# A retrieval layer's walk over 128 expert blocks: split-float matmuls against plain float32, and gathered rows on TensorE against VectorE

## The chip, the cores and the metric

One NeuronCore of a Trainium2 chip runs the whole program. The metric is the device time in microseconds (us) of one execution. PE is TensorE (matmuls; PEld is its weight load), DVE is VectorE, ACT is ScalarE, POOL is GpSimd, SP is SyncE, which here only issues DMAs. "Block" below is a block of 128 experts.

## The reference

Tokens go through a token mixer and a layer norm (not touched here), then through a PEER layer: each token picks 8 x 16 of 16384 experts by two top-16 searches, and its output is a gated sum over them.

```python
def peer_ffn(x, wq, sub_keys, u_tab, v_tab):        # x (512, 1024), tables (16384, 1024) float32
    ...
    s_top, i_top = lax.top_k(scores, PEER_TOPK)
    cand_s = ...; cand_i = i_top[half 0] * 128 + i_top[half 1]
    best_s, best_pos = lax.top_k(cand_s, PEER_TOPK)
    expert_idx = jnp.take_along_axis(cand_i, best_pos, axis=-1)   # (512, 8, 16)
    gates = jax.nn.softmax(best_s, axis=-1)
    def chunk(args):
        xc, ec, gc = args
        u = jnp.take(u_tab, ec, axis=0)
        act = jax.nn.gelu(jnp.einsum("cd,chkd->chk", xc, u)) * gc
        vv = jnp.take(v_tab, ec, axis=0)
        return jnp.einsum("chk,chkd->cd", act, vv)
    ...
x = layer_norm(ALPHA * x + peer_ffn(x, ...), ln2_g, ln2_b)
```

## The kernel before, in words

Everything is float32. The kernel treats the two halves of the 512 tokens in different ways, side by side.

**Dense half (tokens 256 to 511).** A walk over the 128 blocks computes, per block, H = u_block x (a 128x256 result over eight 128-deep steps), its gelu, the product with the block's gates, and adds (gated gelu)^T v_block to four accumulators of 128x512. Each block's u and v (512 KB each) are loaded by SP. A float32 matmul is replaced by three matmuls on split operands, a high part (`fp32r`) and a low part: ACT copies the high part, DVE subtracts for the low part (`split`, lines 115 and 118). So H takes 24 matmuls (`h_run`, L1261) and the output side 12 (`v_tile`, L1253). The first blocks are different already: the output side of blocks 0 to 30 (`NATV = 31`) uses plain float32 on the raw tile (L1243), and H of blocks 6 to 23 does too (`ramp_fill`, L703, with a plain copy of x made by `native_x`). H of the first 24 blocks (`RAMP`) is computed in the ramp, ahead of the walk: between the routing instructions and in the gate stage below.

**Gates of the dense half.** They are made as matmuls of one-hot rows, 32 blocks by 16 tokens at a time: `g_hot` makes four one-hot tensors on DVE, `g_token` 32 small matmuls per group on PE (L972, L973), `g_out` copies them to a ring of 56 blocks on ACT. The first 32 blocks' gates are made in a stage of their own before the walk (16 groups), the other 48 groups in three windows of blocks (`GWIN`: 14 to 31, 38 to 62, 70 to 94) between the walk's matmuls.

**Sparse half (tokens 0 to 255).** Rows of u and v are gathered by indirect DMAs that POOL issues (L1037), 128 rows of 4 KB each. For u, one gather holds slot j of 128 tokens, and DVE forms the 128 dot products in one instruction (`sparse_u`, L1042). For v, one gather holds the 128 slots of one token (`idxT`), and PE adds them up: `sparse_v` multiplies four gathers at a time by columns of coefficients (`expand`, L1102), 8 matmuls of 512 columns. There are 256 gathers of u and 256 of v.

**Order.** Every engine works through its instructions as the program writes them. `work(b, share)` hands a quota of sparse items to block b: 5 a block up to block 13, 3.5 up to block 30, then 383 over 95 blocks, 4.03 a block. `pull` issues gathers as long as fewer than `NGAT = 9` row buffers are held:

```python
    def pull():
        while gq and held[0] < NGAT:
            kind, i, j = gq.popleft()
            t = spare()
            ...
            held[0] += 1
```

A gather therefore waits, on POOL's queue, until the instruction that used the buffer's former content is done. PE meets in block b: H of block b+1, the sparse matmuls that fall there, then the output side of block b, which needs `af` of block b (`a_mul`, L1004, on DVE, behind whatever DVE has in front of it).

## Time and profile before

| what | value |
|---|---|
| device time, 3 runs | 1423.62 us median (1423.08 to 1429.82) |
| the profiled execution | 1420.93 us, its span 1419.1 us |
| PE busy | 1322.5 us, 93% of the span |
| DVE busy | 1086.8 us, 77% |
| POOL busy | 779.0 us, 55% |
| ACT busy | 512.5 us, 36% |
| bytes moved | 439.83 MB, mean 310 GB/s |
| mean granted clock of TensorE | 0.977 of full speed |

The span lasts from the first to the last instruction; the device time has 1.8 us more around it. Busy time of PE includes overlaps of pipelined matmuls, so a busy PE need not be working at its peak. The first 320 us are the mixer and the routing, the walk goes from about 411 to 1392 us.

### The profile page before, as it was taken

The numbers are of one execution on the slowest core, as the hardware profiler recorded it, in microseconds if no ns is written. First come the engines' busy times: TensorE is split into PE (matmuls) and PEld (weight loads), VectorE is DVE, ScalarE is ACT, GpSimd is POOL, SyncE is SP. The second block draws the span as 40 slices with busy tenths as digits, with TensorE's granted clock in tenths as the row PEclk, the third lists the DMA queues.
The fourth block names the chain that finished last, engine by engine and source line by source line (L and its number), as shares of the span: only waits on it lengthen the run. The fifth ranks groups of instructions, "written<-read, shape, count | busy, mean of one in ns | idle before, by whom it ended". The sixth has DMA issues, their size and how long they took to land.

```text
span 1419.1 us, 24250 instructions
## 1 busy us (share of the span) xinstructions
PE 1322.5 (93%) x9229; PEld 1006.2 (71%) x9229; DVE 1086.8 (77%) x2292; ACT 512.5 (36%) x735; POOL 779.0 (55%) x687
## 2 busy tenths in 40 slices
...
GB/s 212 186 63 13 134 84 128 83 75 110 229 199 389 420 411 367 378 375 375 413 377 392 388 385 390 405 419 404 405 403 402 406 364 416 402 419 409 419 408 141
DMA packets 125444, 439.83 MB, mean 310 GB/s; under 512 B 14480, under 2 KB 16528, under 8 KB 125328
## 3 DMA queue, kind: packets, MB, share of 16 engines
...
q14 instruction: 44, 0.36, 0.1%
...
## 4 chain that ended last, share of the span: by engine, by line
PE 50%; issue 14%; DMA 13%; POOL 11%; DVE 10%; ACT 2%; POOLq 0%; DVEq 0%; SPq 0%; ACTq 0%
PE acc L1253 12%; PE w L1261 11%; POOL gat L1037 10%; DMA gat<-in_v,idxT 8%; PE facc L1102 8%; DMA gat<-in_u,idx 4%; PE b L138 4%; PE b L139 4%; PE b L137 4%; PE w L703 3%; DVE i_top L757 2%; DVE s_top L755 1%; PE z L312 1%; DVE sc L760 1%; DVE gat L1042 1%
## 5 line engine op out<-in xcount | busy, mean ns | idle before, releaser
L1037 POOL DMA_INDIRECT gat<-in_u,idx x256 | 336.5, 1314 | 222.5 <-DVE gat L1042 142.6
L1037 POOL DMA_INDIRECT gat<-in_v,idxT x256 | 280.6, 1096 | 178.6 <-PE facc L1102 100.1
L1042 DVE SCALAR_TENSOR_TENSOR gat<-gat,x1s 128x1024 f32<-128x1024 f32 x256 | 309.4, 1222 | 15.7 <-DMA gat<-in_u,idx 15.1
L1253 PE MATMUL acc<-vh,A 128*128 128x512 f32 x768 | 261.5, 401 | 0.0
L1261 PE MATMUL w<-x1Tdh,whi 128*128 128x256 f32 x832 | 241.7, 291 | 1.6 <-ACT gl L1264 1.4
L1261 PE MATMUL w<-x1Tdl,whi 128*128 128x256 f32 x832 | 235.2, 283 | 0.0
L1261 PE MATMUL w<-x1Tdh,wlo 128*128 128x256 f32 x832 | 234.9, 282 | 0.0
L118 DVE TENSOR_TENSOR vl<-vraw,vh 128x1024 fp32r<-128x1024 f32 x96 | 117.5, 1224 | 121.2 <-ACT vh L115 121.1
L1253 PEld LDWEIGHTS acc<-vh,A 128*128 128x128 f32 x768 | 145.1, 189 | 81.5 <-issue 28.5
L1243 PE MATMUL acc<-vraw,af 128*128 128x512 f32 x248 | 136.9, 697 | 48.6 <-DVE af L1004 45.2
L115 ACT ACTIVATE whi<-wraw 128x1024 fp32r<-128x1024 f32 (+1 forms) x146 | 151.0, 1036 | 48.6 <-DMA wraw<-in_wq 25.5
L1102 PE MATMUL facc<-gat,expand 128*32 128x512 f32 x1024 | 152.5, 600 | 14.8 <-DMA gat<-in_v,idxT 14.1
L1261 PEld LDWEIGHTS w<-x1Tdh,whi 128*128 128x128 f32 x832 | 159.4, 192 | 6.1 <-ACT gl L1264 2.3
L1261 PEld LDWEIGHTS w<-x1Tdl,whi 128*128 128x128 f32 x832 | 159.3, 191 | 2.4
L1261 PEld LDWEIGHTS w<-x1Tdh,wlo 128*128 128x128 f32 x832 | 159.0, 191 | 0.0
L118 DVE TENSOR_TENSOR wlo<-wraw,whi 128x1024 fp32r<-128x1024 f32 (+1 forms) x109 | 131.7, 1210 | 34.7 <-ACT whi L115 34.0
L115 ACT ACTIVATE vh<-vraw 128x1024 fp32r<-128x1024 f32 x96 | 101.4, 1056 | 143.5 <-issue 118.1
L1253 PE MATMUL acc<-vl,A 128*128 128x512 f32 x384 | 151.0, 393 | 0.0
L118 POOL TENSOR_TENSOR wlo<-wraw,whi 128x1024 fp32r<-128x1024 f32 x37 | 92.5, 2504 | 96.0 <-ACT whi L115 96.0
L1243 PEld LDWEIGHTS acc<-vraw,af 128*128 128x128 f32 x248 | 51.1, 219 | 112.3 <-DVE af L1004 61.2
L115 ACT ACTIVATE ring<-w 128x384 f32<-128x384 f32 (+2 forms) x80 | 52.4, 740 | 169.4 <-PE w L973 169.4
L1264 ACT ACTIVATE gl<-w 128x256 f32<-128x256 f32 x104 | 39.9, 384 | 185.3 <-PE w L1261 182.8
...
## 6 DMA issues: line engine op xcount, KB each, us to landing
wraw<-in_uT SPq DMA_DIRECT2D x128, 512.0 KB, 8.4
vraw<-in_v SPq DMA_DIRECT2D x128, 512.0 KB, 6.5
wraw<-in_w_in SPq DMA_DIRECT2D x18, 512.0 KB, 3.8
wraw<-in_wq SPq DMA_DIRECT2D x16, 512.0 KB, 3.9
wo<-in_w_out SPq DMA_DIRECT2D x8, 512.0 KB, 9.3
gat<-in_u,idx POOLq DMA_INDIRECT x256, 8.3
gat<-in_v,idxT POOLq DMA_INDIRECT x256, 6.9
...
```

What stands on the lines that cost most here:

```text
L115: return act.activation(o, i, AF.Copy, scale=scale)
L118: eng.tensor_tensor(out=o, in0=a, in1=b, op=OP.subtract)
L137: pe.matmul(ps, lh, rh, start=start, stop=False)
L138: pe.matmul(ps, lh, rl, start=False, stop=False)
L139: pe.matmul(ps, ll, rh, start=False, stop=stop)
L703: pe.matmul(ramp[1], uraw[b][:, k, :], native["x"][:, k, :], start=k == 0, stop=k == 7)
L1037: pool.indirect_dma_start(out=t, out_offset=None, in_=table, in_offset=bass.IndirectOffsetOnAxis(ap=idx, axis=0))
L1042: dve.scalar_tensor_tensor(t, t, 1.0, x1s[i], op0=OP.mult, op1=OP.mult, accum_out=dots[:, j:j + 1])
L1102: pe.matmul(facc[hf][32 * j:32 * j + 32, :], expand[:, j, o:o + 32], ts[j][:, 512 * hf:512 * hf + 512], start=r == 0, stop=r == 31)
L1243: pe.matmul(acc[hf], af[b][:, c:c + 128], raw[:, 512 * hf:512 * hf + 512], start=b == 0, stop=False)
L1253: pe.matmul(acc[hf], lhs[x], rhs[y], start=b == 0 and p == 0, stop=b == NI - 1 and p == 2)
L1261: pe.matmul(ps, w[:, k, :], x1Td[x][:, k, :], start=k == 0 and p == 0, stop=k == 7 and p == 2)
```

## The change

Six things change together.

1. **H of the walk** uses the raw u tile and a plain copy of x: 8 float32 matmuls instead of 24. The splits of u in the walk are gone. `native_x` now writes the plain copy over the split copy of x, so that only blocks 0 to 4 (`RSPL = 5`) use the split one; the rest of them is finished ahead of `native_x`.
2. **The output side** uses the raw v tile for all 128 blocks: 4 float32 matmuls instead of 12. The splits of v and of `af` (the tile `A2`) are gone.
3. **v rows of the sparse half** are gathered by slot like those of u, with the same index tile, and DVE adds coefficient times row to the residual in place (`sparse_v`). `idxT`, its transposes, `expand`, the transposed coefficients and the accumulators `facc` are gone; ACT scales the residual by ALPHA once.
4. **Row buffers** are a list of 18 (12 own ones, four former split tiles, two from the low part of x) and 20 once the ramp's gelu tiles are used up. v has three raw buffers instead of two, and there are two PSUM banks each for H and for gates.
5. **Order in a block**: `a_mul(b)` stands in block b for blocks from 24 on (before: `a_mul(b+1)` in block b, for every block).
6. **Routing**: POOL writes the looked-up products in the order in which they are added up, and DVE adds both of them with one `tensor_reduce` (`add_up`) over adjacent elements; `add_half` is gone. `g_out` writes 16 adjacent tokens at a time.

```diff
-RSPL = 6
+RSPL = 5
-NGAT = 9
-EH = 16
+NGAT = 12
-NATV = 31
...
     def native_x():
...
+            pss.append(ps)
+        x, rows = [xtp.tile([128, 8, ND], FR, name=n).bitcast(F32) for n in ("x1Tdh", "x1Tdl")]
+        for i, ps in enumerate(pss):
+            copy_act(x[:, 2 * i:2 * i + 2, :], ps)
+        native["x"], native["rows"] = x, rows
...
-            pool.tensor_tensor(out=pr, in0=ge, in1=delta[:, :, :, None].to_broadcast([128, NB, TOPK, TOPK]), op=OP.mult)
+            pool.tensor_tensor(out=pr.rearrange("p t s a -> p t a s"), in0=ge, in1=delta[:, :, :, None].to_broadcast([128, NB, TOPK, TOPK]), op=OP.mult)
...
-                dve.tensor_reduce(out=dst, in_=pr.rearrange("p t a s -> p t s a"), axis=AX.X, op=OP.add)
+                dve.tensor_reduce(out=dst, in_=pr, axis=AX.X, op=OP.add)
...
         def route_e(h, pr):
-            add_half(i2A[:, :, h, :], pr)
+            add_up(i2A[:, :, h, :], pr)
...
+        ramp_fill(8 * RSPL - ramp[0])
         native_x()
         ramp_fill(TFILL[0])
...
+    for n in ("whi", "wlo"):
+        for _ in range(2):
+            free.append(wts.tile([128, 8, 128], FR, name=n, bufs=2).bitcast(F32).rearrange("p a c -> p (a c)"))
+    for i in range(2):
+        free.append(native["rows"][:, 4 * i:4 * i + 4, :].rearrange("p a c -> p (a c)"))
+    for i in range(NGAT):
+        free.append(gp.tile([128, D], F32, name=f"gat{i}"))
 
     def pull():
-        while gq and held[0] < NGAT:
+        while gq and free:
...
+    def sparse_v(i, j):
+        t = gats.pop(("v", i, j))
...
+        dve.scalar_tensor_tensor(x1s[i], t, coef[i][:, j:j + 1], x1s[i], op0=OP.mult, op1=OP.add, **more)
...
+        free.append(t)
...
     def v_tile(b, i, slots):
...
         for hf in range(2):
-            cc = slice(512 * hf, 512 * hf + 512)
-            rhs = (vh[:, cc], vl[:, cc])
-            for p, (x, y) in enumerate(((0, 0), (0, 1), (1, 0))):
-                pe.matmul(acc[hf], lhs[x], rhs[y], start=b == 0 and p == 0, stop=b == NI - 1 and p == 2)
-                slots()
+            pe.matmul(acc[hf], af[b][:, c:c + 128], raw[:, 512 * hf:512 * hf + 512], start=b == 0, stop=b == NI - 1)
+            slots(3)
 
     def h_run(b, slots):
-        ps = hbank[:, :ND]
-        (wh, wl) = usplit.pop(b)
+        ps = hbank[b % 2][:, :ND]
+        raw = uraw.pop(b)
         for k in range(8):
-            for p, (w, x) in enumerate(((wh, 0), (wh, 1), (wl, 0))):
-                pe.matmul(ps, w[:, k, :], x1Td[x][:, k, :], start=k == 0 and p == 0, stop=k == 7 and p == 2)
-                slots()
+            pe.matmul(ps, raw[:, k, :], native["x"][:, k, :], start=k == 0, stop=k == 7)
+            slots(3)
...
-        if b + 2 >= RAMP:
-            u_split(b + 2)
-            u_load(b + 4)
+        if b + 3 >= RAMP:
+            u_load(b + 3)
         work(b, 0.25)
-        v_split(b + 1)
-        if b >= NATV:
-            v_load(b + 3)
+        if b >= RAMP:
+            a_mul(b)
...
-        a_mul(b + 1)
-        a_high(b + 1)
+        if b + 1 < RAMP:
+            a_mul(b + 1)
...
-        if b < NATV:
-            v_load(b + 2 + (b == NATV - 1))
+        v_load(b + 3)
```

Three places in the order of instructions, before and after. Names before the arrow are what is written, behind it what is read; line numbers are each kernel's own.

**DVE, about ten blocks before the end of the walk.** Before, two blocks:

```order
L1004 SCALAR_TENSOR_TENSOR af<-gl,ring 128x256
L118 TENSOR_TENSOR A_12402<-af,A_12402 128x256
L118 TENSOR_TENSOR wlo<-wraw,whi 128x1024
L118 TENSOR_TENSOR vl<-vraw,vh 128x1024
L1004 SCALAR_TENSOR_TENSOR af<-gl,ring 128x256
L118 TENSOR_TENSOR A_12473<-af,A_12473 128x256
L118 TENSOR_TENSOR wlo<-wraw,whi 128x1024
L118 TENSOR_TENSOR vl<-vraw,vh 128x1024
```

After, somewhat over two blocks (L1064 is `sparse_v`, L985 is `a_mul`; `whi`, `wlo` and `gat_...` are row buffers):

```order
L985 SCALAR_TENSOR_TENSOR af<-gl,ring 128x256
L1064 SCALAR_TENSOR_TENSOR x1s_85<-gat_3734,coef_4503,x1s_85 128x1024
L1064 SCALAR_TENSOR_TENSOR x1s_85<-glx,coef_4503,x1s_85 128x1024 x2
L1064 SCALAR_TENSOR_TENSOR x1s_85<-gat_3738,coef_4503,x1s_85 128x1024
L985 SCALAR_TENSOR_TENSOR af<-gl,ring 128x256
L1064 SCALAR_TENSOR_TENSOR x1s_85<-gat_3735,coef_4503,x1s_85 128x1024
L1064 SCALAR_TENSOR_TENSOR x1s_85<-whi,coef_4503,x1s_85 128x1024 x2
L1064 SCALAR_TENSOR_TENSOR x1s_85<-wlo,coef_4503,x1s_85 128x1024
L985 SCALAR_TENSOR_TENSOR af<-gl,ring 128x256
L1064 SCALAR_TENSOR_TENSOR x1s_85<-gat_3736,coef_4503,x1s_85 128x1024
L1064 SCALAR_TENSOR_TENSOR x1s_85<-gat_3737,coef_4503,x1s_85 128x1024
L1064 SCALAR_TENSOR_TENSOR x1s_85<-wlo,coef_4503,x1s_85 128x1024
```

Two 128x1024 subtractions and one 128x256 subtraction a block go, about four 128x1024 steps on gathered v rows come.

**PE, late in the walk**, from the end of H of one block to the first part of the next output side. Before (L1102 are the sparse matmuls):

```order
L1261 MATMUL w<-x1Tdh,whi 128x256
L1261 MATMUL w<-x1Tdl,whi 128x256
L1261 MATMUL w<-x1Tdh,wlo 128x256
L1102 MATMUL facc_4540<-gat,expand 32x512 x4
L1102 MATMUL facc_4541<-gat,expand 32x512 x4
L1253 MATMUL acc_0_4536<-vh,A_13753 128x512
L1253 MATMUL acc_0_4536<-vl,A_13753 128x512
L1253 MATMUL acc_0_4536<-vh,A_13753 128x512
L1253 MATMUL acc_1_4537<-vh,A_13753 128x512
L1253 MATMUL acc_1_4537<-vl,A_13753 128x512
```

After, one and a half blocks: H, output side, H (`h_...` and `w` are its two banks), output side:

```order
L1199 MATMUL h_4512<-x1Tdh,wraw 128x256 x8
L1192 MATMUL acc_0_4507<-vraw,af 128x512
L1192 MATMUL acc_1_4508<-vraw,af 128x512
L1192 MATMUL acc_0_4509<-vraw,af 128x512
L1192 MATMUL acc_1_4510<-vraw,af 128x512
L1199 MATMUL w<-x1Tdh,wraw 128x256 x8
L1192 MATMUL acc_0_4507<-vraw,af 128x512
L1192 MATMUL acc_1_4508<-vraw,af 128x512
L1192 MATMUL acc_0_4509<-vraw,af 128x512
L1192 MATMUL acc_1_4510<-vraw,af 128x512
```

The sparse matmuls are gone from PE, and each three matmuls on split parts are one on raw tiles.

**POOL, from the first gather on.** Before:

```order
L1037 DMA gat<-in_u,idx_1552 128x1024 x128
L1037 DMA gat<-in_u,idx_1553 128x1024 x9
L1091 MEMSET expand 128x2172
L1037 DMA gat<-in_u,idx_1553 128x1024 x3
L1037 DMA gat<-in_v,idxT 128x1024 x4
L1037 DMA gat<-in_u,idx_1553 128x1024 x4
L1037 DMA gat<-in_v,idxT 128x1024 x4
L1037 DMA gat<-in_u,idx_1553 128x1024 x4
```

After:

```order
L1008 DMA whi<-in_u,idx_1552 128x1024 x2
L1008 DMA wlo<-in_u,idx_1552 128x1024 x2
L1008 DMA x1Tdl<-in_u,idx_1552 128x1024 x2
L1008 DMA gat_3727<-in_u,idx_1552 128x1024
L1008 DMA gat_3728<-in_u,idx_1552 128x1024
L1008 DMA gat_3729<-in_u,idx_1552 128x1024
```

Nine more, each into a `gat_` buffer of its own, follow directly: the first 18 gathers now find a free buffer instead of the first nine, and the v gathers take the same index tile as those of u.

## Rows read from the trace of the kernel before

**Rows 1.** The page of the profiled execution: busy time, share of the span and number of instructions of each engine (part 1).

```profile
PE 1322.5 (93%) x9229; PEld 1006.2 (71%) x9229; DVE 1086.8 (77%) x2292; ACT 512.5 (36%) x735; POOL 779.0 (55%) x687
```

**Rows 2.** Busy time by stretch, all engines. Columns: stretch and its length, then busy us (and instructions) of PE, PEld, DVE, ACT and POOL, the granted clock of TensorE, the mean busy share of the 16 DMA engines, GB/s.

```profile
205.00:260.00 55.00, 53.79 (x462) 53.59 (x462) 49.73 (x300) 22.88 (x30) 41.86 (x53) 1.00 0.40 129
260.00:317.00 57.00, 50.12 (x417) 48.67 (x415) 56.28 (x327) 16.90 (x25) 41.14 (x55) 1.00 0.26 81
369.00:411.00 42.00, 42.00 (x623) 37.64 (x621) 35.67 (x64) 18.97 (x23) 16.83 (x9) 1.00 0.67 226
411.00:514.00 103.00, 65.36 (x113) 25.25 (x112) 87.11 (x153) 0.38 (x1) 80.91 (x66) 0.83 0.97 384
514.00:638.00 124.00, 111.65 (x855) 70.75 (x856) 120.62 (x208) 29.55 (x50) 81.88 (x61) 0.93 0.99 378
638.00:1148.00 510.00, 491.68 (x3817) 380.01 (x3815) 419.24 (x647) 210.07 (x312) 318.31 (x256) 1.00 1.01 398
1178.00:1392.00 214.00, 214.00 (x1454) 156.44 (x1447) 92.59 (x112) 78.69 (x114) 104.81 (x107) 1.00 1.02 410
1392.00:1419.00 27.00, 13.62 (x81) 10.29 (x79) 15.66 (x33) 8.44 (x15) 0.00 (x0) 0.79 0.19 75
```

**Rows 3.** The same view for line 1004 (`a_mul`, one instruction a block) alone: DVE busy time and, in brackets, how many blocks lie in each stretch; clock, DMA share, GB/s.

```profile
411.00:514.00 103.00, 5.93 (x14) 0.83 0.97 384
514.00:638.00 124.00, 7.12 (x17) 0.93 0.99 378
638.00:1148.00 510.00, 26.84 (x64) 1.00 1.01 398
1148.00:1392.00 244.00, 13.17 (x31) 1.00 1.01 404
```

**Rows 4.** The same view, all engines, for a stretch of 20 us in which the transfers run fastest.

```profile
1160.00:1180.00 20.00, 19.39 (x116) 12.19 (x117) 5.51 (x8) 5.46 (x8) 8.62 (x10) 1.00 1.03 419
```

**Rows 5.** Instructions of PE in order of time, one block late in the walk. Columns: start us, duration us, line, operation, out<-in, shapes, how many in a row.

```profile
1182.46 0.28 PE L1261 MATMUL w<-x1Tdh,whi 128*128 128x256 f32 x1
...
1185.42 1.92 PE L1102 MATMUL facc<-gat,expand 128*32 128x512 f32 x16
1187.27 0.50 PE L1253 MATMUL acc<-vh,A 128*128 128x512 f32 x1
...
1190.12 0.28 PE L1261 MATMUL w<-x1Tdh,whi 128*128 128x256 f32 x1
```

**Rows 6.** Instructions of PE in order of time: plain float32 matmuls of H in the ramp (L703) and of the output in the walk (L1243), each recorded as two instructions, and a bunch of 16 gate matmuls (L972, L973) with the matmul behind it.

```profile
360.53 3.62 PE L703 MATMUL w<-x1Tsh,wraw 128*128 128x256 f32 x16
363.99 0.38 PE L900 MATMUL b<-ident,sc 128*128 128x128 f32 x2
...
593.17 3.60 PE L1243 MATMUL acc<-vraw,af 128*128 128x512 f32 x8
...
1003.63 0.20 PE L972 MATMUL w<-ohAg,ohB 128*128 128x32 f16 x1
...
1004.19 0.36 PE L1261 MATMUL w<-x1Tdh,whi 128*128 128x256 f32 x1
```

**Rows 7.** Instructions of DVE in order of time inside a gate window: the four one-hot instructions of one group of tokens, a step on a gathered u row with its accumulator read, and `a_mul`.

```profile
1019.63 1.22 DVE L957 TENSOR_TENSOR ohB<-i2T,iota 128x2048 f16<-128x2048 f16 x1
1021.90 1.22 DVE L1042 SCALAR_TENSOR_TENSOR gat<-gat,x1s 128x1024 f32<-128x1024 f32 x1
1023.04 0.42 DVE L1004 SCALAR_TENSOR_TENSOR af<-gl,ring 128x256 f32<-128x256 f32 x1
1023.38 1.22 DVE L1042 SCALAR_TENSOR_TENSOR gat<-gat,x1s 128x1024 f32<-128x1024 f32 x1
```

**Rows 8.** Groups of equal instructions: line, engine, operation, out<-in, shapes, count, busy us, mean ns of one, idle time before and what ended it. A 128x1024 step with a scalar pointer (L1134), the subtractions that the splits leave on DVE (L118), and, of the routing, a strided reduction (L799), the first of four halvings (L805) and a contiguous reduction (L908).

```profile
L1134 DVE SCALAR_TENSOR_TENSOR x1s<-x1s,fs,gat 128x1024 f32<-128x1024 f32 x2 | 2.6, 1286 | 2.3 <-ACT gat L1125 2.3
L118 DVE TENSOR_TENSOR wlo<-wraw,whi 128x1024 fp32r<-128x1024 f32 x105 | 129.1, 1230 | 33.2 <-ACT whi L115 32.4 <-PE acc L1253 0.5
L118 DVE TENSOR_TENSOR vl<-vraw,vh 128x1024 fp32r<-128x1024 f32 x96 | 117.5, 1224 | 121.2 <-ACT vh L115 121.1
L799 DVE TENSOR_REDUCE pki<-pr 128x64 int32<-128x1024 f32 x8 | 15.3, 1917 | 0.0
L805 DVE TENSOR_TENSOR pr<-pr 128x512 f16<-128x512 f16 x8 | 7.8, 972 | 0.0
L908 DVE TENSOR_REDUCE sm<-sc 128x32 f32<-128x512 f32 x1 | 0.7, 678 | 0.0
```

**Rows 9.** Gathers issued by POOL, in order of time (start, duration, and in square brackets the idle time before and what ended it): in the gate stage, at the start of the walk, late in the walk.

```profile
387.09 1.96 POOL L1037 DMA_INDIRECT gat<-in_u,idx  x1 [0.30 <-issue]
413.02 1.68 POOL L1037 DMA_INDIRECT gat<-in_u,idx  x1 [23.98 <-DVE gat L1042]
...
1206.77 0.93 POOL L1037 DMA_INDIRECT gat<-in_v,idxT  x1 [0.30 <-issue]
1210.60 0.93 POOL L1037 DMA_INDIRECT gat<-in_v,idxT  x1 [2.90 <-PE facc L1102]
```

**Rows 10.** Busy time of POOL on line 1037 (gathers) in the first 14 blocks: POOL us (instructions), clock, DMA share, GB/s.

```profile
411.00:514.00 103.00, 80.91 (x66) 0.83 0.97 384
```

**Rows 11.** Waits of PE, the largest: what waited, line, what for; us in total, times, longest.

```profile
PE acc L1243 <- DVE af L1004: 45.2, 17, 8.1
```

**Rows 12.** The page's DMA issues (part 6): out<-in, queue, count, KB each, median us from issue to landing.

```profile
vraw<-in_v SPq DMA_DIRECT2D x128, 512.0 KB, 6.5
```

208 lines of the change are left out of this document (71 added, 137 removed).

## The prediction

> **What bounds the kernel now.** I read the shares first, then the busy time stretch by stretch, then single blocks. PE's 93% of the span [rows 1] is a mean over stages with different limits. In the gate stage (369 to 411) PE is busy all 42.00 us [rows 2]. The blocks are counted by `a_mul` [rows 3]. Blocks 0 to 13 (411 to 514) are not PE's: 65.36 of 103 us. DVE has 87.11 us, and POOL 80.91 us in 66 gathers; with the 0.30 us of issue ahead of each [rows 9] that is 80.91 + 66 x 0.30 = 101 of 103 us [rows 2, 10]. POOL is full because it starts late: the tenth gather goes out at 413.02, after 23.98 us of waiting for a u step to free one of nine buffers [rows 9]. The transfers run at 384 GB/s there, against 419 at their best [rows 2, 4]. Blocks 14 to 30 take 124 us with DVE at 120.62. Blocks 31 to 94 take 510 us, 7.97 a block, with PE at 491.68; blocks 95 to 125 take 244 us, 7.87 a block, with PE busy for 214.00 of the 214 us to 1392 [rows 2, 3]. There PE is the bound; its late block lasts 1190.12 - 1182.46 = 7.66 us: H 2.96, sparse matmuls 1.85, output side 2.85 [rows 5]. The transfers stand close behind, at 398 and 404 to 410 GB/s [rows 2, 3].
>
> **The change, part by part.** The sum goes against the profiled execution, 1420.9 us, which is 2.7 below the median of the three runs.
>
> *PE.* In plain float32 eight H matmuls take 363.99 - 360.53 = 3.46 us, and the output side of a block 3.60 us with its modelled end [rows 6]; I take 3.44, the pitch H shows, since both have the same number of columns. The walk's PE block becomes 6.90 us (7.06 at most) instead of 7.66: the two float32 parts cost 1.1 us more and the 1.85 us of sparse matmuls go. A group of gates adds two bunches of 1004.19 - 1003.63 = 0.56 us, about 1.2 with their gaps [rows 6]; 32 groups lie in blocks 31 to 94.
>
> *DVE.* The subtractions go (117.5 and 129.1 us [rows 8], mostly in the walk) and 256 v steps come. No v step is in this trace; the nearest rows are a u step, 1.22 us long at a pitch of 1023.04 - 1021.90 = 1.14 us [rows 7], and a step with a scalar pointer, 1.286 us [rows 8]. I take 1.25, range 1.14 to 1.29, and `a_mul` at 0.34 and four one-hot instructions at 2.27 [rows 7]. Blocks 0 to 30 hold 129 sparse items, all u but one. Blocks 31 to 94 hold 258, half of them v.
>
> *Transfers.* Bytes stay the same, 4.03 + 2 pieces of 0.524 MB in a late block = 3.16 MB, but nine more gathers (4.7 MB) leave in the gate stage, where only 226 GB/s run [rows 2]. At the gate stage's pitch of 1.96 + 0.30 us [rows 9] eighteen gathers take 41 us of its 42.
>
> *Stage by stage.*
> - Routing and gate stage. The strided reduction (1917 ns) becomes contiguous; from 678 ns for half the elements [rows 8] I estimate 1.36 us: 0.56 less, eight times. Four halvings (972 ns and at most half as much again and again, under 1.94 us) become one such reduction: up to 0.6 less, eight times. PE's idle time between 205 and 317, 1.2 + 6.9 us [rows 2], bounds the gain at 8 us. Against it: one split H block becomes plain (+0.5 us), PE waits for ACT's copies over `x1Tdh` before the fill matmuls (no row shows it; 0 if they keep ahead of PE, 3 if it waits for most of the four), and POOL's product of the same size writes strided, which may cost nothing or double its 2 us a head. Value -3, ends -8 and +8.
> - Blocks 0 to 30, 227 us now. Floors after: transfers 103 x 0.384 + 124 x 0.378 = 86.4 MB, less 4.7, at 418 GB/s = 195 us; DVE 129 x 1.14 + 31 x 0.34 + 16 x 2.27 = 194 us; PE in blocks 14 to 30, where eight H are due, 17 x 3.44 + 8 x 3.46 + 16 x 1.2 = 105 us at full clock, 113 at the granted 0.93 [rows 2]. POOL has 111 gathers left at 1.5 us (103 / 66), 167 us, and is no bound. Three near-equal floors never overlap wholly: 204, or -23 (ends 197 and 215).
> - Blocks 31 to 94, 510 us now. PE 64 x 6.90 + 32 x 1.2 = 480 (490 with 7.06). Transfers 510 x 0.398 = 203 MB, 484 us at 419 GB/s, 495 at 410. DVE 127 x 1.14 + 131 x 1.25 + 64 x 0.34 + 32 x 2.27 = 403. Value 490, or -20 (ends 482 and 510).
> - Blocks 95 to 125, 244 us now. Transfers 244 x 0.404 = 98.6 MB, 235 us at 419, 240 at 410; PE 31 x 6.90 = 214; DVE 125 x 1.25 + 31 x 0.34 = 167. The transfers are the bound: 237, or -7 (ends 233 and 244).
> - Tail, 27 us: the last H and output sides at plain pitch and no split to prepare, finish steps as before: +3 (ends 0 and +5).
>
> Sum -3 - 23 - 20 - 7 + 3 = -50: 1371 us by the profile, 1372 asked for here. What hides the loss of 1.1 us a block on PE's float32 parts is the removed 1.85 us of sparse matmuls; without that cover blocks 31 to 125 would cost 95 x 1.1 = 105 us. `a_mul(b)` now stands in block b behind about four DVE steps, so a late gathered row holds DVE, then `a_mul`, then the output side queued on PE, and every H behind it; v raw has three buffers, so `v_load` is next in line to be late.
>
> **The rivals.**
>
> *R1, transfers alone.* If 18 to 20 buffers keep the queues full, everything after the gate stage runs at 419 GB/s: 389 MB less 4.7 is 917 us, from 408 to 1325, and 28 us of tail: 1353; with 8 us gained in the routing, 1345. For it: the late stretches reach 410 to 419 already [rows 2, 4]. Against: PE needs as long in blocks 31 to 94.
>
> *R2, coupling.* PE lost 45.2 us to `af` in the early blocks [rows 11]. If the order in a block costs PE 0.3 to 0.5 us for `af` in each of 95 blocks, 29 to 48 us return: 1395 to 1420. For it: `a_mul` behind gathered rows. Against: `af` has three buffers, and DVE has a fifth of its time free.
>
> *R3, slower: POOL's gathers get slow.* A gather's issue costs 0.93 us late in the walk, with little on DVE, and 1.68 to 1.96 at the start of the walk and in the gate stage [rows 9], where DVE is busy for 85% [rows 2]. After the change DVE runs v steps with two tensor inputs all through the walk. At the gate stage's 2.26 us a gather, 383 gathers take 866 us in blocks 31 to 125 instead of 754, and 111 take 251 in blocks 0 to 30: 408 + 251 + 866 + 30 = 1555. It decides above (1419 - 408 - 30) / 494 = 1.99 us a gather. Against: in blocks 0 to 13, with DVE at 85%, the pitch is 1.5, and 4.03 x 1.5 = 6.0 us a block is under 7.5; the subtractions that go had two inputs as well and took about as long. The Trainium skill bears on this (SBUF — State Buffer, "SBUF: two separate sides"): DVE with two SBUF inputs, against a GpSimd instruction that reads SBUF, and GpSimd take one port pair as an exclusive lock, held for a whole instruction, while the other blocks fully. Read strictly, each gather could wait out a whole v step, and the time would be the one just given. The trace agrees in kind, 0.93 against 1.96 us, but does not show a full step added at the 1.5 us pitch.
>
> *R4, slower: a dear v step.* If the in-place sum took over (781 - 250) / 254 = 2.09 us, DVE's 127 x 1.14 + 95 x 0.34 + 32 x 2.27 = 250 us and 254 v steps would eat all gains (781 = 754 and the 27 us gained elsewhere). Against: the nearest rows say 1.29 at most.
>
> *R5, slower: loads behind gathers.* With 18 gathers queued, a u or v load could land late; v loads land in 6.5 us [rows 12], and one issued three blocks (22 us) ahead has room to spare. It would need more than 15 us.
>
> **How the numbers follow.** My forecast 0.60 (1355 to 1393, likeliest 1372), R1 0.17 (1338 to 1355), R2 0.13 (1393 to 1425), R3 0.05 (1450 to 1555), R4 and R5 together 0.05 (1425 to 1480). A measurement here can tell 0.5%, 7 us, from no change: faster (below 1416) 0.60 + 0.17 + 0.09 = 0.86, same 0.04, slower 0.10. The range 1343 to 1408 leaves out about 0.04 below and 0.16 above, which is where R2's end and the slower cases lie.
>
> **What the profile after would show.** Right: eighteen gathers back to back before the walk; block 0 at about 408, block 31 at 612, block 95 at 1102, the end of block 125 at 1339; transfers at 410 to 419 GB/s from the first block to the last; PE at 6.9 us a block; v steps of 1.14 to 1.29 us; POOL's gathers at 1.0 to 1.5 us. Wrong: PE waiting for `af` in most late blocks (R2); POOL full at 2 us a gather and DVE waiting for rows that were issued late (R3); DVE full with v steps of 2 us (R4); PE waiting for `wraw` or `vraw` (R5); a first block after 411 would void the routing term.

## The result, and the profile after

The changed kernel takes 1366.76 us, the median of 4 runs (1364.74 to 1369.49), against 1424.42 us (1423.08 to 1429.82) of the kernel before: a ratio of 0.9588, 95% interval 0.9558 to 0.9618. The profiled execution spans 1367.7 us, 51.4 less than before. The forecast was 1372 us.

The page after, parts 1 and 2 (shares of the engines; GB/s in 40 slices of the span), beside [rows 1]:

```profile
PE 1292.5 (94%) x6973; PEld 916.1 (67%) x6973; DVE 1110.9 (81%) x2219; ACT 247.7 (18%) x428; POOL 842.5 (62%) x685
...
GB/s 213 200 51 27 138 31 156 100 87 87 214 317 329 374 416 353 369 414 419 420 418 420 418 419 419 419 420 418 418 420 418 419 418 416 414 419 419 419 419 186
```

PE is as busy as before in its share. From slice 18 on the transfers run at 414 to 420 GB/s in every full slice.

Busy time by stretch after, columns as in [rows 2]. The last five stretches are cut where the first output matmul of blocks 0, 14, 24, 31, 95 and 126 starts:

```profile
205.00:260.00 55.00, 53.63 (x461) 53.44 (x461) 48.30 (x307) 22.75 (x30) 43.94 (x59) 1.00 0.41 130
260.00:317.00 57.00, 55.83 (x474) 55.21 (x474) 56.52 (x348) 16.30 (x24) 40.73 (x54) 1.00 0.30 90
369.00:411.00 42.00, 41.79 (x615) 36.56 (x615) 37.07 (x68) 11.95 (x23) 28.89 (x16) 1.00 0.89 328
408.00:505.50 97.50, 62.62 (x115) 24.07 (x113) 87.00 (x156) 0.39 (x1) 78.81 (x57) 0.86 0.95 364
505.50:578.00 72.50, 63.39 (x448) 35.83 (x449) 72.12 (x132) 6.97 (x21) 60.61 (x40) 0.88 0.97 363
578.00:633.00 55.00, 55.00 (x346) 37.92 (x345) 43.65 (x79) 7.78 (x21) 45.52 (x32) 1.00 1.02 416
633.00:1113.00 480.00, 480.00 (x2561) 326.77 (x2560) 403.67 (x577) 49.74 (x119) 313.03 (x253) 1.00 1.03 419
1113.00:1350.70 237.70, 223.69 (x747) 141.56 (x746) 166.80 (x156) 12.26 (x32) 154.49 (x115) 0.99 1.00 408
```

From block 31 on PE has no idle time for 480 us, and the transfers stand at 419 GB/s at the same time. The 7 blocks 24 to 30 are PE's as well (55.00 of 55). Blocks 14 to 23 are DVE's: 72.12 of 72.5 us.

PE in order of time after, without gate work (start, duration, line, operation, tiles, count), early and late in the second half; L1199 is H, L1192 the output side, beside [rows 5]:

```profile
643.49 3.62 PE L1199 MATMUL w<-x1Tdh,wraw 128*128 128x256 f32 x16
646.95 3.60 PE L1192 MATMUL acc<-vraw,af 128*128 128x512 f32 x8
650.38 3.62 PE L1199 MATMUL h<-x1Tdh,wraw 128*128 128x256 f32 x16
...
1182.00 3.62 PE L1199 MATMUL w<-x1Tdh,wraw 128*128 128x256 f32 x16
1185.97 3.70 PE L1192 MATMUL acc<-vraw,af 128*128 128x512 f32 x8 [0.35 <-DVE af L985]
1189.50 3.62 PE L1199 MATMUL h<-x1Tdh,wraw 128*128 128x256 f32 x16
```

A block is 650.38 - 643.49 = 6.89 us long, H 3.46 and output 3.43, as the prediction took from [rows 6]. In the last quarter the same two steps stand 1189.50 - 1182.00 = 7.50 us apart, with a gap ahead of the output side that `af` ends. What `af` waits for is in DVE's rows (with the idle time before, and the group of the v steps on `gat` buffers):

```profile
1187.57 1.28 DVE L1064 SCALAR_TENSOR_TENSOR x1s<-gat,coef,x1s 128x1024 f32<-128x1024 f32 x1 [0.46 <-DMA gat<-in_v,idx]
1190.05 1.28 DVE L1064 SCALAR_TENSOR_TENSOR x1s<-wlo,coef,x1s 128x1024 f32<-128x1024 f32 x1 [1.20 <-DMA wlo<-in_v,idx]
...
L1064 DVE SCALAR_TENSOR_TENSOR x1s<-gat,coef,x1s 128x1024 f32<-128x1024 f32 x151 | 193.9, 1284 | 46.9 <-DMA gat<-in_v,idx 46.0
```

DVE waits for gathered rows: the transfers set the pace there, 3.16 MB / 0.419 = 7.54 us a block. A v step lasts 1284 ns, at the upper end of what was forecast.

For every kernel of this text the table gives the stages in us, cut at the start of the first output matmul of blocks 0, 14, 31, 95 and 126, so that the sum of a row is the span. (The prediction cut at `a_mul`, which the change moves against the matmuls; the sums are the same.)

| kernel | to block 0 | 0 to 13 | 14 to 30 | 31 to 94 | 95 to 125 | rest | span |
|---|---|---|---|---|---|---|---|
| before | 411.7 | 103.6 | 127.9 | 519.1 | 237.7 | 19.1 | 1419.1 |
| after | 408.3 | 97.3 | 127.6 | 480.1 | 237.5 | 16.9 | 1367.7 |
| e1_nine | 408.8 | 101.5 | 127.6 | 479.7 | 231.8 | 20.9 | 1370.3 |
| e2_psum | 410.2 | 90.2 | 135.6 | 480.0 | 226.0 | 16.9 | 1358.9 |
| e3_halfu | 408.4 | 87.8 | 117.1 | 480.1 | 239.4 | 16.9 | 1349.7 |
| e4_halfh | 409.7 | 96.4 | 124.3 | 478.2 | 237.8 | 19.5 | 1365.9 |
| e5_psall | 407.3 | 99.4 | 128.0 | 479.7 | 225.7 | 17.2 | 1357.3 |
| e6_early | 408.5 | 92.0 | 134.2 | 479.7 | 224.9 | 15.8 | 1355.1 |
| e7_outf32 | 411.5 | 102.5 | 123.4 | 535.0 | 257.6 | 19.7 | 1449.7 |
| e8_vdve | 411.9 | 106.1 | 127.9 | 565.7 | 246.0 | 23.3 | 1480.9 |
| e9_outf13 | 412.0 | 104.5 | 123.3 | 517.4 | 256.8 | 18.7 | 1432.7 |
| e10_ahead | 406.6 | 96.4 | 120.9 | 479.7 | 227.1 | 15.7 | 1346.4 |
| e11_route | 415.8 | 96.6 | 127.4 | 480.1 | 237.5 | 17.0 | 1374.4 |
| e12_amul | 406.8 | 96.6 | 127.6 | 479.7 | 239.7 | 16.9 | 1367.3 |

So 39 of the 51 us came out of blocks 31 to 94, 6 out of blocks 0 to 13, 3 ahead of block 0, 2 behind block 125, and nothing out of blocks 14 to 30 and 95 to 125. The whole is right; where the gain lies is not where the prediction put it, and the experiments are about that.

POOL's gathers after, beside [rows 9] (start, duration, idle time before):

```profile
387.47 1.96 POOL L1008 DMA_INDIRECT gat<-in_u,idx  x1 [0.30 <-issue]
398.80 1.97 POOL L1008 DMA_INDIRECT gat<-in_u,idx  x1 [0.30 <-issue]
409.61 1.68 POOL L1008 DMA_INDIRECT whi<-in_u,idx  x1 [8.84 <-DVE whi L1013]
...
431.28 1.98 POOL L1008 DMA_INDIRECT gat<-in_u,idx  x1 [0.30 <-DMA gat<-in_u,idx]
433.56 1.99 POOL L1008 DMA_INDIRECT gat<-in_u,idx  x1 [0.30 <-issue]
435.86 1.19 POOL L1008 DMA_INDIRECT gat<-in_u,idx  x1 [0.30 <-issue]
```

The gathers of the gate stage go out back to back at 2.27 us, the eighteenth at 398.80, then POOL waits 8.84 us for the first u step. Behind it the gathers take 1.98 us again, two of three, although these are blocks with no gate work. POOL's time on gathers in blocks 0 to 30:

```profile
408.30:633.20 224.90, 184.94 (x127) 0.90 0.98 376
```

With the 0.30 us of issue ahead of each gather that is the whole stretch: from 418 to 633 us no gather waits for a free buffer.

### The profile page after: what moved, and what is told of

Its sections match the earlier page's. It is cut to its first block, busy times and chain, and to the rows that moved or that the text cites. A ratio compares the mean times of both kernels' runs of the same rounds, so it can differ in the third digit from the quotient of the medians.

```text
span 1367.7 us, 19187 instructions
## 1 busy us (share of the span) xinstructions
PE 1292.5 (94%) x6973; PEld 916.1 (67%) x6973; DVE 1110.9 (81%) x2219; ACT 247.7 (18%) x428; POOL 842.5 (62%) x685
## 4 chain that ended last, share of the span: by engine, by line
PE 57%; DMA 18%; DVE 11%; issue 7%; POOL 6%; ACT 1%; SPq 0%; DVEq 0%; POOLq 0%
PE acc L1192 17%; DMA gat<-in_v,idx 9%; PE w L1199 9%; PE h L1199 9%; DMA glx<-in_v,idx 4%; PE b L136 4%; PE b L137 4%; PE b L135 4%; POOL gat L1008 4%; PE w L700 3%; DVE gat L1013 2%; DMA gat<-in_u,idx 2%; DVE i_top L757 1%; DMA wlo<-in_v,idx 1%; DMA whi<-in_v,idx 1%
## 5 line engine op out<-in xcount | busy, mean ns | idle before, releaser
L1192 PE MATMUL acc<-vraw,af 128*128 128x512 f32 x1024 | 487.8, 620 | 55.3 <-DVE af L985 55.3
L1192 PEld LDWEIGHTS acc<-vraw,af 128*128 128x128 f32 x1024 | 197.7, 198 | 273.3 <-issue 191.9
L1008 POOL DMA_INDIRECT gat<-in_v,idx x151 | 194.9, 1291 | 86.0 <-issue 31.3
L1064 DVE SCALAR_TENSOR_TENSOR x1s<-gat,coef,x1s 128x1024 f32<-128x1024 f32 x151 | 193.9, 1284 | 46.9 <-DMA gat<-in_v,idx 46.0
L1013 DVE SCALAR_TENSOR_TENSOR gat<-gat,x1s 128x1024 f32<-128x1024 f32 x159 | 191.4, 1222 | 10.8 <-DMA gat<-in_u,idx 10.4
L1199 PE MATMUL h<-x1Tdh,wraw 128*128 128x256 f32 x832 | 196.2, 386 | 2.7 <-DMA wraw<-in_uT 2.7
L1199 PE MATMUL w<-x1Tdh,wraw 128*128 128x256 f32 x832 | 194.7, 383 | 0.0
L1199 PEld LDWEIGHTS h<-x1Tdh,wraw 128*128 128x128 f32 x832 | 156.6, 192 | 35.9 <-issue 17.9
L1199 PEld LDWEIGHTS w<-x1Tdh,wraw 128*128 128x128 f32 x832 | 155.5, 191 | 33.1 <-issue 15.6
L116 POOL TENSOR_TENSOR wlo<-wraw,whi 128x1024 fp32r<-128x1024 f32 x36 | 90.2, 2509 | 97.7 <-ACT whi L113 97.7
L985 DVE SCALAR_TENSOR_TENSOR af<-gl,ring 128x256 f32<-128x256 f32 x104 | 44.2, 425 | 60.7 <-ACT gl L1202 58.1
L965 PEld LDWEIGHTS <-ohB 128*128 128x128 f16 x1024 | 73.7, 117 | 24.6 <-issue 19.0
L964 PEld LDWEIGHTS <-ohB 128*128 128x128 f16 x1024 | 79.3, 117 | 15.8 <-issue 14.4
L1202 ACT ACTIVATE gl<-h 128x256 f32<-128x256 f32 x52 | 19.9, 383 | 286.4 <-PE h L1199 278.7
L1202 ACT ACTIVATE gl<-w 128x256 f32<-128x256 f32 x52 | 19.9, 383 | 284.5 <-PE w L1199 278.0
L700 PE MATMUL w<-x1Tdh,wraw 128*128 128x256 f32 x304 | 70.3, 384 | 0.6 <-ACT x1Tdh L113 0.6
L700 PEld LDWEIGHTS w<-x1Tdh,wraw 128*128 128x128 f32 x304 | 56.4, 191 | 7.5 <-ACT x1Tdh L113 0.8
```

Of the source, the lines that this page charges most:

```text
L116: eng.tensor_tensor(out=o, in0=a, in1=b, op=OP.subtract)
L700: pe.matmul(ramp[1], uraw[b][:, k, :], native["x"][:, k, :], start=k == 0, stop=k == 7)
L964: pe.matmul(ps[:, t, :], B[:, g, :, f], Ag[:, g, :SG, f], start=True, stop=False)
L965: pe.matmul(ps[:, t, :], B[:, g, :, f], Ag[:, g, SG:, f], start=False, stop=True)
L1008: pool.indirect_dma_start(out=t, out_offset=None, in_=u if kind == "u" else v, in_offset=bass.IndirectOffsetOnAxis(ap=idxs[i][:, j:j + 1], ...
L1013: dve.scalar_tensor_tensor(t, t, 1.0, x1s[i], op0=OP.mult, op1=OP.mult, accum_out=dots[i][:, j:j + 1])
```

## Experiments

The kernel before took 1428.98 us beside e1 to e4, 1433.97 beside e5 to e8 and 1426.96 beside e9 to e12, so the ratios to it are compared, and the changed kernel's is 0.9588.

**What holds blocks 0 to 30, and what it costs.** First POOL and DVE. In e2 a copy of the first 128 tokens' x stands in PSUM:

```diff
...
-        dve.scalar_tensor_tensor(t, t, 1.0, x1s[i], op0=OP.mult, op1=OP.mult, accum_out=dots[i][:, j:j + 1])
+        x = pair if i == 0 and NPS[0] <= j < NPS[1] else x1s[i]
+        dve.scalar_tensor_tensor(t, t, 1.0, x, op0=OP.mult, op1=OP.mult, accum_out=dots[i][:, j:j + 1])
...
+    pair = pacc.tile([128, D], F32, name="pair")
+    hbank = [pair[:, :512], pair[:, 512:]]
...
+    copy_act(pair, x1s[0])
```

> The changed kernel with one edit: 94 of the first 128 u steps (blocks 1 to 21) read the tokens' x from a copy in PSUM instead of SBUF, so that DVE's step has one SBUF input; DVE's work per step stays. Theory C (blocks 0 to 30 are held back by POOL, whose gathers take 1.98 us while DVE runs steps with two SBUF inputs): gathers between 410 and 560 us take about 0.95 to 1.2 us, transfers reach 400 to 419 GB/s in 415 to 505 us instead of 350 to 391, block 14 starts its output side near 492 instead of 505.6, the whole takes 1345 to 1357 us. Rival D (DVE's own 198 us of work is the bound and POOL's slow gathers follow from nothing that matters): 1364 to 1370 us, blocks 0 to 30 still 219 to 225 us, whatever the gathers take. Third, a PSUM operand may cost DVE something: a step longer than 1.3 us would make it slower than 1367.

1357.59 us, ratio 0.9491 (0.9458 to 0.9523): faster than the changed kernel, the intervals do not overlap. Three gathers of e2 in a row, at the time of the last three above:

```profile
433.09 0.93 POOL L1009 DMA_INDIRECT gat<-in_u,idx  x1 [0.30 <-issue]
434.35 0.93 POOL L1009 DMA_INDIRECT gat<-in_u,idx  x1 [0.33 <-issue]
435.60 0.94 POOL L1009 DMA_INDIRECT whi<-in_u,idx  x1 [0.32 <-DVE wlo L1015]
```

The groups of gathers into `gat` buffers and of u steps in 411 to 505 us (count, busy us, mean ns), of the changed kernel and then of e2:

```profile
L1008 POOL DMA_INDIRECT gat<-in_u,idx x36 | 48.7, 1353 | 11.0 <-issue 10.1 <-DMA gat<-in_u,idx 0.6 <-DMA whi<-in_u,idx 0.3
L1013 DVE SCALAR_TENSOR_TENSOR gat<-gat,x1s 128x1024 f32<-128x1024 f32 x44 | 52.3, 1226 | 5.5 <-DMA gat<-in_u,idx 5.2
```

```profile
L1009 POOL DMA_INDIRECT gat<-in_u,idx x39 | 36.8, 943 | 20.2 <-issue 7.9 <-DVE gat L1015 4.0 <-DVE af L986 3.0
L1015 DVE SCALAR_TENSOR_TENSOR gat<-gat,pair 128x1024 f32<-128x1024 f32 x47 | 55.2, 1212 | 3.5 <-DMA gat<-in_u,idx 2.7 <-issue 0.8
```

DVE's step is the same (1226 and 1212 ns), and from 430 to 460 us it runs without a pause in e2. In these steps only the place of one operand differs, and the mean gather falls from 1353 to 943 ns. So it is not that DVE is busy, but that it reads two SBUF tensors, which makes two of three of POOL's gathers twice as long: theory C's mechanism is shown. The Trainium skill (SBUF — State Buffer, "SBUF: two separate sides") names this condition, two SBUF inputs, for its lock on a port pair; the measured 1.04 us that such a gather is longer (1.98 against 0.94) is close to the 1.14 us pitch of a step, as a lock held for a whole instruction would give. Not every gather waits that long: others take 1.19 or 1.68 us.

Where the gain appears is another matter. Blocks 0 to 30 last 225.8 us in e2, not less than the 224.9 of the changed kernel, and 12 us go from blocks 95 to 125. The busy times of two stretches show what links the two; changed kernel, e2, and e3 below:

```profile
430.00:460.00 30.00, 19.04 (x37) 7.61 (x38) 26.89 (x48) 0.00 (x0) 25.12 (x17) 0.91 0.98 350
530.00:560.00 30.00, 23.73 (x179) 12.51 (x177) 29.83 (x56) 3.29 (x10) 25.12 (x17) 0.89 0.95 346
```

```profile
430.00:460.00 30.00, 21.58 (x44) 8.10 (x42) 30.00 (x56) 0.00 (x0) 17.87 (x20) 0.94 1.03 419
530.00:560.00 30.00, 23.34 (x152) 12.05 (x151) 23.05 (x43) 2.53 (x8) 16.08 (x17) 0.85 1.01 403
```

```profile
430.00:460.00 30.00, 16.65 (x28) 6.55 (x29) 13.95 (x40) 0.00 (x0) 18.33 (x19) 0.86 1.03 419
530.00:560.00 30.00, 28.32 (x212) 18.00 (x213) 24.52 (x62) 3.40 (x10) 22.20 (x19) 1.00 1.03 418
```

The last figure of a row is the rate of the transfers: 350 and 346 GB/s, 419 and 403, 419 and 418. Over 405 to 627 us e2 moved 4.8 MB more than the changed kernel, worth 11.4 us at 419 GB/s, and its span is 8.8 us shorter (its ratio says 14). Bytes that POOL issues late in blocks 0 to 30 are paid for in blocks 95 to 125, where the transfers are the last to be done. That e2 did not start block 31 sooner is due to three blocks: it was 7.0 us ahead up to block 17 (110.9 us from block 0, against 117.9), then blocks 17 to 19 took 28.1 us instead of 20.2, with DVE busy for 23.05 us of 530 to 560 and idle times on PE and DVE for which the profile names no releaser. What held them stays open.

e3 halves DVE's u steps of these blocks:

```diff
-        dve.scalar_tensor_tensor(t, t, 1.0, x1s[i], op0=OP.mult, op1=OP.mult, accum_out=dots[i][:, j:j + 1])
+        c = 512 if i == 0 else D
+        dve.scalar_tensor_tensor(t[:, :c], t[:, :c], 1.0, x1s[i][:, :c], op0=OP.mult, op1=OP.mult, accum_out=dots[i][:, j:j + 1])
```

> The changed kernel with the 128 u steps of blocks 0 to 30 on the first 512 of 1024 columns (half of each dot product is left out); the gathers are whole. Theories C and D (DVE, by its time or by what it does to POOL): blocks 0 to 30 fall from 219 to 195 to 205 us, where the transfers at 419 GB/s and PE stop them, the whole takes 1342 to 1355 us. Rival E (the gathered transfers are slow in these blocks for a reason of their own): no change, 1362 to 1370 us, and 350 to 380 GB/s there as before.

1350.32 us, ratio 0.9449 (0.9415 to 0.9483). Blocks 0 to 30 fall to 204.9 us, and 8.0 MB more are moved by 627 us (19 us; the span falls by 18). Rival E is out: the transfers reach 418 to 420 GB/s as soon as DVE and POOL let them. So DVE's steps hold these blocks back, and the bytes that their hold on POOL leaves unmoved are paid for later (C). How much of block 31's start is DVE's own time (D) and how much its hold on POOL is not separated: e3 shortens both at once, and in the changed kernel DVE and POOL are both full.

**The bound from block 31 on.** e4 leaves out half of H from block 32 on:

```diff
-        for k in range(8):
+        nk = 8 if b < 32 else 4
+        for k in range(nk):
...
```

> The changed kernel with four instead of eight H matmuls for each block from 32 on (half of each H sum is left out): PE's block falls by 1.73 us to 5.2. Theory F (from block 31 on the transfers at 419 GB/s are a bound of their own): blocks 31 to 94 stay at 475 to 482 us, blocks 95 to 125 at 234 to 240, transfers at 419 to 422 GB/s, the whole 1358 to 1368 us. Rival G (PE paces, and the transfers only follow it): blocks 31 to 94 fall by 64 x 1.73 = 110 us towards 370 to 420, transfers go above 430 GB/s, the whole under 1300 us.

```profile
630.40:1108.60 478.20, 402.20 (x2049) 235.94 (x2048) 401.94 (x574) 50.20 (x120) 314.90 (x251) 0.95 1.03 419
1108.60:1346.00 237.40, 185.26 (x496) 98.36 (x496) 169.38 (x158) 11.98 (x32) 152.63 (x118) 0.91 1.02 414
```

1366.98 us, ratio 0.9566: no change, with PE down to 402 of 478 us. The transfers are a bound of their own from block 31 on (F), and PE's 480 us in blocks 31 to 94 lie exactly beside the 478 us that they take here.

**Are the buffers what keeps them there?** e1 takes nine of the 18 to 20 away:

```diff
-NGAT = 12
+NGAT = 9
...
-    for n in ("whi", "wlo"):
-        for _ in range(2):
-            free.append(wts.tile([128, 8, 128], FR, name=n, bufs=2).bitcast(F32).rearrange("p a c -> p (a c)"))
-    for i in range(2):
-        free.append(native["rows"][:, 4 * i:4 * i + 4, :].rearrange("p a c -> p (a c)"))
...
-        if b + 1 == RAMP:
-            for i in range((RAMP - RSLOT) * ND // D):
-                free.append(glx[:, D * i:D * i + D])
...
```

> The changed kernel with 9 row buffers, as before the change, instead of 18 to 20. Theory A (the number of buffers is what keeps the transfers at 419 GB/s): transfers fall to about 400 GB/s in blocks 31 to 94 (480 us become 500), the first gathers again stop after nine, the whole takes 1390 to 1405 us. Rival B (only PE's shorter block made the gain; buffers are idle): 1366 to 1375 us, transfers still at 415 or more from block 31 on.

```profile
638.00:1117.00 479.00, 479.00 (x2559) 325.26 (x2558) 401.91 (x574) 49.84 (x119) 310.73 (x252) 1.00 1.03 419
```

1374.52 us, ratio 0.9626 (0.9597 to 0.9655): its interval overlaps that of the changed kernel, so the buffers are worth some 5 us, within 0 to 11, and not 20 or more. 419 GB/s with nine buffers: rival B. Nine fewer early gathers (4.7 MB, 11 us at 419 GB/s) were made up in part: from 430 to 460 us DVE, short of rows, was busy for 25.57 us instead of 26.89, and POOL got out 21 gathers instead of 17 (419 GB/s instead of 350); by 627 us 134.8 MB were moved, against 137.4.

**One part at a time, on the kernel before.** e7 is the kernel before with `NATV = 128`, the output side in plain float32 for every block.

> The kernel before with one part of the change alone: the output side in plain float32 for all 128 blocks (no splits of v and af). PE's late block goes from 7.66 to 7.66 - 2.85 + 3.44 = 8.25 us. Theory (PE bounds blocks 31 to 125 before the change, and the removed sparse matmuls are what pays for float32): 95 x 0.59 = 56 us slower, 1478 to 1490 us. Rival (the splits that leave DVE and ACT give more than PE loses, since DVE waited 121 us for vh): 1400 to 1435.

```profile
637.00:1172.00 535.00, 524.90 (x3618) 335.79 (x3618) 321.67 (x520) 127.17 (x192) 324.82 (x263) 0.99 0.99 386
1172.00:1430.00 258.00, 258.00 (x1473) 150.61 (x1473) 48.33 (x59) 39.67 (x62) 118.24 (x114) 1.00 0.96 366
```

1448.79 us, ratio 1.0087 (1.0058 to 1.0116): slower, but by some 12 us instead of 56. (The profiled run, 1451.75 us, is the longest of its seven, and the median of before's runs beside it is 13 us above the profiled execution of before; so stages are compared here, not spans.) In blocks 95 to 125 the step is as worked out (19.9 us more for 31 blocks, 0.64 each); in blocks 31 to 94 it costs 15.9 us instead of 38. PE was therefore not the bound of that stage before the change. One sees why in the order of work: only half of its 258 items are v rows, so a block holds half a sparse group on average, and PE's work was 64 x 5.81 + 33 x 1.85 + 32 x 1.2 = 471 us, not 510.

e9 gives e7 13 buffers from block 0 on (`turn_g` sends four of every 13 rows to a tile of their own, `gat2`):

```diff
...
+        if turn_g[1] and turn_g[0] % 13 >= 9:
+            return mp2.tile([128, D], F32, name="gat2", bufs=4)
...
-        while gq and held[0] < NGAT:
+        while gq and held[0] < NGAT + turn_g[1]:
```

> Like e7_outf32 (output side in plain float32, sparse matmuls still on PE), with 13 row buffers from the start of the walk instead of 9. Theory H (before the change blocks 31 to 94 were not bound by PE's work, about 7.4 us a block with half a sparse group, but by v rows that come and go four at a time through nine buffers): the stage falls from 535 us towards PE's 64 x (6.40 + 0.95 + 0.6) = 509, and the whole by 15 to 30 us against e7_outf32, ratio to before 0.99 or less. Rival I (PE's own work bounds it): blocks 31 to 94 stay within 5 us of 535, ratio 1.005 to 1.012.

```profile
640.00:1157.00 517.00, 514.79 (x3617) 333.68 (x3615) 320.18 (x520) 127.18 (x191) 324.02 (x260) 1.00 1.00 395
1157.00:1414.00 257.00, 257.00 (x1476) 150.47 (x1473) 49.31 (x60) 39.55 (x62) 116.27 (x113) 1.00 0.95 368
```

1435.35 us, ratio 1.0070 (1.0036 to 1.0104). The stage falls from 535.0 to 517.4 us, two thirds of the way to PE's 509, though 6.8 us of that lie in a single block (block 32: 17.8 us in e7, 11.0 here); the whole, by its ratio, does not differ measurably from e7. The stage leans to H, the total settles nothing.

PE's sparse matmuls in blocks 31 to 94 show what kept these blocks above PE's work. First the kernel before: all 544 of them (busy us, mean ns and, behind the bar, idle time before them), then one group from its first matmul to the output side behind it. Second all 544 in e9:

```profile
L1102 PE MATMUL facc<-gat,expand 128*32 128x512 f32 x544 | 93.0, 600 | 14.6 <-DMA gat<-in_v,idxT 13.9 <-ACT expand L115 0.7
656.66 2.16 PE L1102 MATMUL facc<-gat,expand 128*32 128x512 f32 x4
...
663.84 0.50 PE L1253 MATMUL acc<-vh,A 128*128 128x512 f32 x1
```

```profile
L1108 PE MATMUL facc<-gat,expand 128*32 128x512 f32 x544 | 67.3, 599 | 1.7 <-DMA gat<-in_v,idxT 1.1 <-ACT expand L115 0.7
```

This group takes 663.84 - 656.66 = 7.18 us instead of 1.85 [rows 5], because its rows land while PE stands at it. The 544 matmuls cost 93.0 + 14.6 = 107.6 us before the change and 69.0 us with 13 buffers (85.5 in e7): the kernel before lost 38.6 us here to v rows that came late, part of it hidden in PE's busy time. Without that loss its stage would be 519.1 - 38.6 = 480.5 us (an estimate), and the changed kernel, whose PE has no sparse matmuls, takes 480.1. So by these profiles the 39 us of this stage are waits for v rows that are gone; PE's own work is about the same as before. In e7 rows leave four at a time, when PE is through with a group, and nine buffers hold two such groups; in e1 they leave one by one, and nine are enough. The kernel before itself with more buffers wasn't tried, as its split tiles take the room.

e8 is the other half: v summed by DVE on the kernel before, splits kept.

```diff
...
-            table, idx = (u, idxs[i][:, j:j + 1]) if kind == "u" else (v, idxT[:, 128 * i + j:128 * i + j + 1])
+            table, idx = (u, idxs[i][:, j:j + 1]) if kind == "u" else (v, idxs[i][:, j:j + 1])
...
+        dve.scalar_tensor_tensor(x1s[i], t, coef[i][:, j:j + 1], x1s[i], op0=OP.mult, op1=OP.add, **more)
...
```

> The kernel before with the other part alone: v rows gathered by slot and summed by DVE, no sparse matmuls, splits of u, v and af kept, 9 buffers. PE's late block falls to about 5.8 us. Theory (the splits had to go because DVE could not carry both): DVE needs 127 x 1.14 + 131 x 1.25 + 64 x (0.34 + 0.42 + 2 x 1.23) + 73 = 587 us in blocks 31 to 94 and 256 us in blocks 95 to 125 instead of 510 and 244: 1500 to 1520 us. Rival (taking the sparse matmuls off PE is what makes the gain, and the transfers then bound): 1370 to 1395.

```profile
646.00:1211.00 565.00, 452.71 (x3329) 393.96 (x3327) 562.08 (x770) 202.59 (x305) 369.27 (x255) 0.89 0.96 357
1211.00:1457.00 246.00, 203.89 (x1114) 169.65 (x1115) 243.87 (x253) 84.17 (x129) 178.53 (x121) 0.93 1.01 398
```

1481.92 us, ratio 1.032 (1.0267 to 1.0372). DVE is busy 562 of 565 us: the theory, at 566 and 246 us instead of 587 and 256. Each half alone loses, one to PE and one to DVE; together PE's sparse matmuls pay for float32, and the splits that go pay for the v steps.

**The routing.** e11 undoes the routing of part 6 (the order of POOL's products too; `g_out` stays as changed):

```diff
...
-                dve.tensor_reduce(out=dst, in_=pr, axis=AX.X, op=OP.add)
+                dve.tensor_reduce(out=dst, in_=pr.rearrange("p t a s -> p t s a"), axis=AX.X, op=OP.add)
...
-            add_up(i2A[:, :, h, :], pr)
+            add_half(i2A[:, :, h, :], pr)
...
```

> The changed kernel with the routing as before (products written in their old order, strided reduction and halvings). Theory (the routing part was worth about 3 us): the first output side starts 2 to 5 us later than 408.3, near 411.5, the whole 2 to 5 us longer than the changed kernel's. Rival (POOL's strided write costs what DVE gains): start within 1 us of 408.3.

Stretch 205 to 317, a reduction of DVE and POOL's product, of the changed kernel; then the stretch of e11:

```profile
205.00:317.00 112.00, 109.46 (x933) 108.65 (x933) 104.83 (x653) 39.05 (x54) 84.67 (x113) 1.00 0.35 110
L799 DVE TENSOR_REDUCE pki<-pr 128x64 int32<-128x1024 f32 x8 | 9.6, 1200 | 0.0
L794 POOL TENSOR_TENSOR pr<-ge,dl 128x1024 f32<-128x1024 f16 x16 | 31.8, 1987 | 25.9 <-DVE ge L791 25.9
```

```profile
205.00:317.00 112.00, 103.95 (x877) 102.33 (x876) 103.86 (x611) 37.96 (x53) 81.21 (x111) 1.00 0.32 105
```

1375.95 us, ratio 0.9654 (0.9613 to 0.9696). Block 0 starts 7.5 us later than after the change: the routing of part 6 was worth 7.5 us, more than expected, and the other edits ahead of the walk cost about 4 (408.3 + 7.5 is 4.1 later than before's 411.7). PE is busy 109.46 us instead of 103.95 of the 112. POOL's strided write costs next to nothing (1987 ns, 1940 in e11).

**The place of `a_mul`.** e12 has `a_mul(b + 1)` in block b throughout.

> The changed kernel with a_mul(b + 1) in block b for every block, as before the change. Theory (PE does not wait for af from block 31 on, whichever place it has): the whole within 4 us of the changed kernel, ratio 0.956 to 0.962, no PE wait for af after block 31. Rival (DVE then waits for the gelu of the H just made, as it does for 51 us in blocks 31 to 94 already, and its steps come later): 5 to 15 us longer.

1369.21 us, ratio 0.9607 (0.9566 to 0.9648), every stage within 2.2 us: part 5 is worth nothing that can be measured. PE does not wait for `af` in blocks 31 to 94, as expected; behind them it does, for 7.0 us, against 11.3 in the changed kernel.

**Further along the same line.** e5 keeps x in PSUM for all of blocks 1 to 30 (one bank each for H and gates):

```diff
...
+    hbank = [psw.tile([128, 512], F32, name="w")] * 2
+    gbank = [psw.tile([128, 512], F32, name="w")] * 2
...
```

> Like e2_psum, with the copy of x kept in PSUM for all u steps of blocks 1 to 30 (H and gates share one bank each instead of two). Theory C with the rule that the time follows the bytes moved before block 31 (e2_psum moved 4.9 MB more by 627 us, 12 us at 419 GB/s, and gained 12): e2_psum still ran at 366 to 407 GB/s in 560 to 627; filling that gives 2.4 MB or 4 to 6 us, so 1351 to 1355 us, transfers at 405 or more up to 627. Rival: the one-hot steps of the gate window (two SBUF inputs) are what slows the gathers there, or the single banks make PE wait: 1357 to 1362.

1356.93 us, ratio 0.9440 (0.9400 to 0.9480), not separable from e2. The transfers were at 384 and 369 GB/s in 560 to 627, less than expected. From block 24 on, the row buffers were full (POOL waits some 24 us for DVE to free them), and a block of PE's 8.11 us asks for (3.5 + 2) x 0.524 = 2.88 MB only, 356 GB/s. Earlier PE waited for v loads:

```profile
PE acc L1196 <- DMA vraw<-in_v: 20.4, 4, 7.4
```

A price of saturated transfers that e2 did not show.

e6 does four u steps ahead of the first `a_mul`:

```diff
     pull()
+    for _ in range(4):
+        sparse.popleft()[1]()
+        pull()
     a_mul(0)
```

> Like e5_psall, with the first four u steps ahead of the first a_mul on DVE, which waits 4.4 us there for the last gates. Theory (transfers that stand idle before the walk are lost for good): the 19th gather goes out near 405 instead of 410 us, four gathers (2.1 MB) earlier, 3 to 5 us faster than e5_psall. Rival: the first output side is delayed by as much as DVE starts later (PE waits for af of block 0): no gain, within 2 us of e5_psall.

```profile
404.75 1.68 POOL L1009 DMA_INDIRECT whi<-in_u,idx  x1 [4.00 <-DVE whi L1015]
```

The nineteenth gather goes out at 404.75 instead of 409.61, as expected, and the first output side is not later (408.5). 1357.26 us, ratio 0.9452 (0.9415 to 0.9489): no gain that can be told from e5.

e10 adds H of four blocks where PE is idle:

```diff
+AHEAD = (4, 6, 8, 10)
...
-        run_h = RAMP <= b + 1 < NI - 1
+        run_h = RAMP + len(AHEAD) <= b + 1 < NI - 1
...
+        if b in AHEAD:
+            i = RAMP + AHEAD.index(b)
+            u_load(i)
+            h_run(i, lambda n: None)
+            u_load(i + 2)
...
```

> Like e6_early, with H of blocks 24 to 27 in blocks 4, 6, 8 and 10, where PE waits for the transfers, instead of blocks 23 to 26 (four more tiles for gelu). Theory (blocks 22 to 30 run at PE's 8.1 us: H 3.46, output 3.44, gates 1.2; PE's floor from there to the end is now the bound): blocks 22 to 26 fall to 6.5 to 7 us, block 31 starts 5 to 8 us earlier and so does the end, 1349 to 1353 us. Rival (the transfers have no slack left, so what PE gains is waited for in blocks 95 to 125): within 2 us of e6_early's ratio, 0.9452.

The transfers of e10 (GB/s in 40 slices):

```profile
GB/s 217 203 52 28 141 24 162 88 90 86 185 329 401 419 420 419 419 418 419 419 419 419 419 419 419 419 419 418 418 419 419 416 419 419 413 419 419 418 419 167
```

1348.48 us, ratio 0.9471 (0.9436 to 0.9506). Blocks 14 to 30 fall from 134.2 to 120.9 us and block 31 starts 10.8 us earlier than in e6. Of the 13.3 us, blocks 22 to 26, which the edit aims at, give 5.0 (7.3 us each, not 6.5 to 7); block 16 alone gives 8.4 (14.4 us in e6, with PE idle and no releaser that the profile names, 6.0 here), which the edit does not explain. The span of e10, 1346.4, is the shortest of all whole kernels. By its ratio e10 is not faster than e6, so that the last step is open; that it beats both kernels, the changed one by about 1.2% (0.9471 against 0.9588), is clear.

## Why the prediction was right, step by step

- *The sum* said -50, the spans say -51.4, and that they agree so closely is luck. By the prediction's own marks (`a_mul` of blocks 0, 31, 95 and 126) the times were 407.8, 626.9, 1107.3 and 1347.5, against 408, 612, 1102 and 1339: blocks 0 to 30 took 15 us more than forecast, blocks 31 to 94 and the rest behind the last mark 10 us less each.
- *Routing and gate stage, -3:* -3.4, as the sum of +4 and -7.5 (e11). The contiguous reduction takes 1200 ns instead of the estimated 1360, and PE's idle time, named as the bound of 8 us, was used for 5.5 us in that stretch.
- *Blocks 0 to 30, 204 us:* 219 (225 between output sides); this term failed, with two steps in it. It took floors of whole stages (195, 194, 113), while the bound changes inside: blocks 1 to 6 take 6.1 us each (DVE, 5 x 1.14 + 0.34), blocks 10 to 12 take 7.5 (transfers), 14 to 21 6.2 to 7.2 (DVE with one-hot steps, 6.6), 23 to 28 8.1 (PE, 6.90 + 1.2); these 23 blocks take 162 us, and the other eight 63. And it let POOL off with "111 gathers left at 1.5 us", "and is no bound": with rows at hand DVE runs two-input steps back to back, and a gather takes up to 1.98 + 0.30 (e2); and the rows gathered ahead for later blocks were left out, so that 127 gathers fell into these blocks and filled POOL. (Their 129 items are all u steps, not "all u but one"; the sums count them so.) The eighteen early gathers came as forecast; of the 11 us that nine more of them are worth, some 3 us by the spans and 5 by the ratios were left at the end (e1).
- *Blocks 31 to 94, 490 us:* 480. The value lay between the floors and allowed 10 us for overlap; none was lost, PE's 480 and the transfers' 478 simply coincide (e4). The reading of before was wrong, though: "There PE is the bound" held for blocks 95 to 125, not here, where a block had half a sparse group (e7). PE's 491.68 us of busy time were taken for work, while 38.6 us of the stage were waits for v rows (e9). So the gain of this stage, 39 us by output sides, is not PE's shorter block (471, or 480 by the rows, to 480 is none), but those waits.
- *Blocks 95 to 125, 237 us:* 240 (237.5 by output sides, as before). Transfer-bound as said, but they had to make up what was not moved earlier.
- *Tail, +3:* -2.2 by output sides (-5.9 by the prediction's marks, since `a_mul` of the last blocks was moved); the f32 tail was no longer than the one with the last splits. The v step, 1.25 forecast, is 1.28.
- *The rivals.* R1 (transfers alone) did not come, but e10 with 413 to 420 GB/s from slice 14 on is what it described, 1346 against its 1345 to 1353. R2's wait for `af` is there late (11.3 us), as the last link of a wait for rows. R3's mechanism is real and its price was far too high: at 1.76 us a gather with its issue over blocks 0 to 30 POOL stays below its 1.99, though it has no time to spare there. R4 did not come, R5 only in e5.
